# Prompt attention: value sums of two neighbouring key blocks issued as one run, six buffers of transposed weights, values loaded in pieces

## The chip, the cores and the metric

The kernel runs on one core of a Trainium2 chip. The metric is the device time of one launch in microseconds (us), as the median of three runs.

## The reference

One hybrid decoder layer for a prompt of 2048 tokens and for 32 sample tokens (8 sequences of 4). The layer normalises its input, multiplies it by one wide projection, feeds four groups (convolution, pooling, stick-breaking attention, attention to memory tokens), gates each, projects the result back and adds it to the residual. The change is in the stick-breaking attention of the prompt, 8 heads of 64:

```python
def sb_block(q, k, v, bias, q_pos, k_pos):
    z = (jnp.einsum('nqhd,nkhd->nhqk', q, k).astype(jnp.float32) * (SB_HEAD_DIM ** -0.5)
         + bias.astype(jnp.float32)[None, :, None, None])
    mask = (k_pos[None, :] < q_pos[:, None])[None, None]
    log_beta = jax.nn.log_sigmoid(z)
    log_1m = jnp.where(mask, jax.nn.log_sigmoid(-z), 0.0)
    rc = lax.cumsum(log_1m, axis=3, reverse=True)
    a = jnp.exp(jnp.where(mask, log_beta + rc - log_1m, -jnp.inf))
    return jnp.einsum('nhqk,nkhd->nqhd', a.astype(v.dtype), v)
```

In products instead of logarithms: the weight of a key is sigmoid(z) times the product of sigmoid(-z) over all later keys that the query may see.

## The kernel before

The kernel first projects the prompt and the sample tokens, with the sample's attention to its cache interleaved, then does prompt attention (about 1502 to 1990 us of the profile), and then the output projection. Queries, keys, values and gates go through DRAM scratch (`qd`, `kd`, `vd`, `gsd`) between the first two.

Prompt attention goes over 16 blocks: 4 head pairs `hp` by 4 query blocks `qb` of 512 tokens. Within a block it goes over key blocks `kc` of 512 from the diagonal down to 0, so there are 40 (block, `kc`) groups. Each group has four steps: two heads `hh` by two halves `q2` of the query block. The work of a step by engine:

- PE, `score` (L1248): four matmuls into a two-bank PSUM tile `S` (two buffers).
- ACT (L1253, L1255): two sigmoids of `S`, into `gam` (three tiles, used in turn) and `be`.
- DVE (L1265 on the diagonal, L1268 off it): two reversed running products of `gam` into `E`, with the carry from the key block before.
- POOL (L1277): two products of `be` and `E`, into `be`.

These two last parts (`rest`) are issued two steps after their score. Then, from a list sorted by step:

- `turn` (L1288): for each of four 128-key blocks `r` and each head, up to four PE transposes of the weights into a PSUM tile `AT` (two buffers), and a copy to the SBUF tile `at`, by ACT off the diagonal (L1294), by DVE with the mask on it (L1292). Both heads of block `r` go at step `base + r + 6`, where `base` is the group's first step.
- `values` (L1304): for block `r`, one product with the values for each head, the two heads side by side in halves of 64 columns of the array, all added into one PSUM tile `av` (one buffer). Each product is two PE instructions, so a call gives four. It goes at `base + r + 8`. After the last block of `kc` 0, DVE multiplies `av` by the gate `sgt` into `sbo` (L1309), and a DMA stores it.

The order of PE's instructions is that of the program (`manual_schedule` for PE). Those of the other engines and of the DMA queue are laid out by the framework's scheduler, which also sets the waits. Within one step of the sorted list older entries come first: values of block `r` come ahead of the transposes of block `r + 2`.

`load` (L1195 to L1211) is called one block ahead. It loads `Q` and `kT` of the block, and, at the first query block of a head pair, all 2048 tokens of the pair's values as one 1 MB tile `V` (two buffers). All of these DMAs are on SP's queue. Other work (sample attention to memory, the rest of the convolution, weights of the output projection) is mixed in through a generator of side work that takes its turns by the costs that `sb_prompt` yields; it uses ACT, DVE, POOL and SP, and the `AT` tiles.

Of the kernel before, what the change touches and what calls it, by code (L numbers as in the profile page):

```python
# [8 lines left out]
F32 = mybir.dt.float32  # L9
# [9 lines left out]
P = 128  # L19
# [39 lines left out]
SEND = 0.97  # L59
XA = 3  # L60
KT = 2
WR = 2


# [22 lines left out]
def kernel(  # L87
# [9 lines left out]
    pe, act, dve, pool, sp = nc.tensor, nc.scalar, nc.vector, nc.gpsimd, nc.sync  # L97
# [22 lines left out]
    vd = dram.tile([SEQ, 512], F32, name="vd")  # L120
# [7 lines left out]
    def mix_rows(ct, t0, n):  # L128

        return mixd[ct // 4, t0 // P : (t0 + n) // P, :, ct % 4].rearrange("b p t -> p b t")  # L130

    def by_tile(t):
        return t.rearrange("p (b t) -> p b t", t=P)
# [88 lines left out]
    def load_w(it):  # L222
        part, kind, c = it
        src, o = (w_mem0, P * c) if kind == "mem" else (w_in0, G[kind] + P * c)
        raw_ = wp.tile([P, ND, P], F32, tag="wr", name="wr%d%s%d" % it, bufs=WR)
        wq.dma_start(raw_, src[:, o : o + P].rearrange("(d p) n -> p d n", p=P))
        return raw_

    def split_w(raw, nm):
        lo = wp.tile([P, ND, P], F32R, tag="wlo", name=f"wlo{nm}", bufs=2)  # L230
        hi = wp.tile([P, ND, P], F32R, tag="whi", name=f"whi{nm}", bufs=2)
        act.copy(hi, raw)
        pool.tensor_tensor(out=lo, in0=raw, in1=hi.bitcast(F32), op=ALU.subtract)
        return hi, lo
# [505 lines left out]
    def next_raw():  # L740
        if SEQ_W:
            it = SEQ_W.pop(0)
            raw[it] = load_w(it)

    def fill_w(n=2):

        while len(wsplit) < n and (raw or SEQ_W):
# [3 lines left out]
            wsplit[it] = split_w(raw.pop(it), "%d%s%d" % it)  # L751
        while n == 2 and len(raw) < WR and SEQ_W:
            next_raw()
# [137 lines left out]
    def gather(dst, rows, idx):  # L891
        pool.indirect_dma_start(out=dst, out_offset=None, in_=rows, in_offset=bass.IndirectOffsetOnAxis(ap=idx, axis=0))  # L892

    def sample_stages(sm, sps, S):
# [8 lines left out]
        def page(n, ml):  # L903
            return NPAGE - 2 - 2 * (n % NCK) + ml

        def load_k(n, ml):
            if n < N:
                kt = sm.tile([P, 4 * 512], F32, tag="kt", name=f"kt{n}_{ml}", bufs=KT)
                gather(kt, krows, S["idk"][:, n // NCK, page(n, ml) : page(n, ml) + 1])
# [281 lines left out]
    def sb_loader(sbr):  # L1191

        KT, V = {}, {}

        def load(hp, qb):  # L1195
            tok = slice(512 * qb, 512 * qb + 512)
            Q = []
            for hh in range(2):
                pr = slice(64 * hh, 64 * hh + 64)
                kt = sbr.tile([P, 512], F32R, tag="kT", name=f"kT{hp}_{qb}_{hh}", bufs=10)  # L1200
                qt_ = sbr.tile([P, 2, 512], F32R, tag="Q", name=f"Q{hp}_{qb}_{hh}", bufs=4)
                for x in range(2):
                    hx = slice(64 * x, 64 * x + 64)
                    sp.dma_start(kt[hx].bitcast(F32), kd[hp, pr, x, tok])
                    sp.dma_start(qt_[hx].bitcast(F32), qd[hp, pr, :, tok])
                KT[hp, hh, qb] = kt
                Q.append(qt_)
            if qb == 0:
                V[hp] = sbr.tile([P, 16, P], F32, tag="V", name=f"V{hp}", bufs=2)
                sp.dma_start(V[hp], vd[:, P * hp : P * (hp + 1)].rearrange("(t p) c -> p t c", p=P))  # L1210
            return Q, KT, V[hp]  # L1211

        return load

    def sb_prompt(load, loaded, sb, bps, ops, flags):
# [18 lines left out]
        A, avs, ats = {}, {}, {}  # L1234
        count = {"pair": 0}

        def score(hp, qb, kc, hh, q2, Q, KT, carry):

# [7 lines left out]
            for j in range(2):  # L1246
                for x in range(2):
                    pe.matmul(S[:, j, :w], lhsT=Q[hh][:, x, P * (q2 + j) : P * (q2 + j + 1)], rhs=KT[hp, hh, kc][:, :w],  # L1248
                              start=x == 0, stop=x == 1)
# [32 lines left out]
        def turn(hp, qb, kc, r, hh):  # L1282
            dg = kc == qb
            q0 = r if dg else 0
            nm = f"{hp}_{qb}_{kc}_{r}_{hh}"
            ap_ = bps.tile([P, 512], F32, tag="AT", name=f"AT{nm}", bufs=2)
            for qt in range(q0, 4):
                pe.transpose(ap_[:, P * qt : P * (qt + 1)], A[hp, qb, kc, hh, qt][:, P * r : P * (r + 1)], ident)  # L1288
            at = sb.tile([P, 512], F32, tag="at", name=f"at{nm}", bufs=4)
            c = slice(P * q0, 512)  # L1290
            if dg:
                dve.tensor_tensor(out=at[:, c], in0=ap_[:, c], in1=tri[:, : 512 - P * q0], op=ALU.mult)  # L1292
            else:
                act.copy(at[:, c], ap_[:, c])  # L1294
            ats[hp, qb, kc, r, hh] = at

        def values(hp, qb, kc, r, V, gt):
            dg = kc == qb
            c = slice(P * r if dg else 0, 512)
            if dg and r == 0:  # L1300
                avs[hp, qb] = bps.tile([P, 512], F32, tag="av", name=f"av{hp}_{qb}", bufs=1)
            av = avs[hp, qb]
            for hh in range(2):
                pe.matmul(av[64 * hh : 64 * hh + 64, c], lhsT=V[:, 4 * kc + r, 64 * hh : 64 * hh + 64],  # L1304
                          rhs=ats.pop((hp, qb, kc, r, hh))[:, c], start=dg and r == 0, stop=kc == 0 and r == 3,
                          tile_position=(0, 64 * hh))
            if kc == 0 and r == 3:
                mo = sb.tile([P, 512], F32, tag="sbo", name=f"sbo{hp}_{qb}", bufs=1)
                dve.tensor_tensor(out=mo, in0=av, in1=gt, op=ALU.mult)  # L1309
                (pool if (hp, qb) == blocks[-1] else sp).dma_start(mix_rows(8 + hp, 512 * qb, 512), by_tile(mo))  # L1310
                flags.add((hp, qb))

        late, pend = [], []
        step = 0

        def behind(limit):
            while late and late[0][0] <= limit:
                late.pop(0)[1]()

        for bi, (hp, qb) in enumerate(blocks):  # L1320
            if bi + 1 < len(blocks) and blocks[bi + 1] not in loaded:
                loaded[blocks[bi + 1]] = load(*blocks[bi + 1])
            Q, KT, V = loaded[hp, qb]
            gt = sb.tile([P, 512], F32, tag="sgt", name=f"sgt{hp}_{qb}", bufs=1)
            sp.dma_start(gt, gsd[hp, :, 512 * qb : 512 * qb + 512])
            carry = {}
            for kc in range(qb, -1, -1):
                base = step
                for hh in range(2):
                    for q2 in (0, 2):  # L1330
                        cost = 1.33 * (2 * q2 + 3) / 4 if kc == qb else 2.66
                        rest = score(hp, qb, kc, hh, q2, Q, KT, carry)
                        if len(pend) == 2:
                            pend.pop(0)()
                        pend.append(rest)
                        yield cost / 2
                        behind(step)
                        step += 1
                        yield cost / 2
                for r in range(4):  # L1340
                    late.append((base + r + 6, lambda a=(hp, qb, kc, r, 0): turn(*a)))
                    late.append((base + r + 6, lambda a=(hp, qb, kc, r, 1): turn(*a)))
                    late.append((base + r + 8, lambda a=(hp, qb, kc, r, V, gt): values(*a)))
                late.sort(key=lambda x: x[0])
        flags.add("last")
        while late:
# [453 lines left out]
    sbr = bx = None  # L1800
    for cost in main():
        tasks.step()
        due += rate * cost
        while sample is not None and due >= 1.0:
            due -= 1.0
            try:
# [5 lines left out]
                sbr = bx.enter_context(tc.tile_pool(name="sbr", bufs=1, side="right", reuse_waits="tile"))  # L1812
# [5 lines left out]
    sb = bx.enter_context(tc.tile_pool(name="sbl", bufs=1, side="right", reuse_waits="tile"))  # L1818
# [81 lines left out]
    for cost in sb_prompt(load, blk, sb, bps, ops, flags):  # L1900
        steps += 1
        if steps > SLATE:
            due += cost
            while side is not None and due >= PACE:
                due -= PACE
                try:
                    next(side)
                except StopIteration:
                    side = None
        if "last" in flags and side is None:  # L1910
            if lead is None:
                os_.close()
                accp = oy.enter_context(tc.tile_pool(name="oacc", bufs=1, space=PSUM, side="left", reuse_waits="tile"))
                lead = leading()
            for _ in range(LPACE):
                next(lead, None)
# [148 lines left out]
```

## Time and profile before

| | us |
|---|---|
| median of 3 runs | 2429.65 (2429.42 to 2430.13) |
| profiled execution, span from the first to the last instruction | 2426.4 |
| what the median has beside that span | 3.25 |
| of it prompt attention, first score matmul to last value matmul | 1502.8 to 1990.5 |

The profile is of one execution. PE is the tensor engine's matmuls, PEld its weight loads, which overlap matmuls; DVE, ACT, POOL and SP are the vector, scalar, GpSimd and sync engines. A timeline row has the start and length in us, the engine, the line, the instruction, the tiles out<-in, the shapes, the number of like instructions merged into the row, and, in brackets, the idle time of the engine ahead of it with what ended that time. Instructions of PE and ACT overlap their neighbours, so the pace of an engine is read from start to start and not from the lengths.

### The profile page before, as it was taken

Reading aid. Unit: us, or ns where it says so; the run is one execution under the profiler, and the core shown is the slowest. Engines: PE = TensorE matmul, PEld = TensorE weight load, DVE = VectorE, ACT = ScalarE, POOL = GpSimd, SP = SyncE. Lnnn points to the kernel's source line nnn. Section 1 sums busy time; section 2 is a strip of 40 time slices with the busy share of each in tenths; the row PEclk is TensorE's granted clock in tenths of the full one; section 3 lists DMA queues with packets and bytes.
Section 4 is the critical chain, followed back from the end, with each engine's and each line's share of the span. In section 5 each row is a group of like instructions: output and inputs, shape, how many; then the busy total and the mean of one; then the engine's idle time right before and its main releaser. Section 6 shows DMA issues by size and latency. Waiting matters only on the chain. (4 is left out here: it accounts for less than half of the span.)

```text
span 2426.4 us, 42151 instructions
## 1 busy us (share of the span) xinstructions
PE 2290.7 (94%) x15962; PEld 1776.1 (73%) x15962; DVE 1736.2 (72%) x2434; ACT 1118.5 (46%) x1939; POOL 1272.7 (52%) x1309
## 2 busy tenths in 40 slices
PE   6999999999999999999999999899999998989997
PEld 6998888898887777777777776455555556777775
DVE  5332784969756665477877877888898857886898
ACT  5322343242442322124241425688989955543444
POOL 2554545556574455655555554576876844433330
PEclk9999999999999999999999999999999999999998
DMA  5678988887778799987877776834332227887764
GB/s 184 213 253 285 350 290 292 290 263 265 261 253 275 271 346 329 312 285 253 290 265 271 260 239 164 239 81 118 101 88 73 63 63 239 272 279 254 238 240 161
DMA packets 340438, 562.15 MB, mean 232 GB/s; under 512 B 28481, under 2 KB 212929, under 8 KB 323834
## 3 DMA queue, kind: packets, MB, share of 16 engines
q1 hardware_dynamic: 284858, 290.72, 39.1%
q0 software_dynamic: 55376, 268.72, 31.1%
q8 instruction: 126, 2.06, 0.3%
q14 instruction: 78, 0.64, 0.1%
HBM read 469.28 MB, written 90.68 MB: 231 GB/s over the span
## 5 line engine op out<-in xcount | busy, mean ns | idle before, releaser
L925 DVE STREAM_TRANSPOSE T<-kt 128x1024 f32<-128x1024 f32 x256 | 308.8, 1226 | 193.6 <-PE sSA L938 183.0
L892 POOL DMA_INDIRECT vt<-in_cache_v_dram,idv x256 | 250.4, 978 | 239.7 <-PE sO L977 178.8
L583 DVE SCALAR_TENSOR_TENSOR cacc<-U,par,cacc 128x512 f32<-128x512 f32 x480 | 360.1, 750 | 11.8
L1277 POOL TENSOR_TENSOR be<-be,E 128x512 f32<-128x512 f32 (+2 forms) x320 | 303.5, 956 | 117.0 <-DVE E L1268 52.6
L1268 DVE TENSOR_TENSOR_SCAN E<-gam,cr,ZM 128x513 f32<-128x513 f32 x192 | 232.9, 1262 | 14.4 <-ACT gam L1253 13.2
L892 POOL DMA_INDIRECT kt<-in_cache_k_dram,idk x128 | 125.6, 981 | 206.9 <-DVE T L925 152.5
L1288 PEld LDWEIGHTS AT<-ident,be 128*128 128x128 f32 x1088 | 117.9, 142 | 127.3 <-ACT at L1294 45.3
L1885 PE MATMUL acc<-wohi,mh 128*128 128x512 f32 (+1 forms) x480 | 193.6, 403 | 3.9 <-DVE mh L1650 2.0
L1253 ACT ACTIVATE gam<-S,nbias_bc 128x1024 f32<-128x1024 f32 (+1 forms) x160 | 172.5, 1078 | 51.2 <-ACT be L1255 18.9
L1885 PE MATMUL acc<-wolo,mh 128*128 128x512 f32 (+1 forms) x480 | 190.8, 397 | 0.0
L1885 PE MATMUL acc<-wohi,ml 128*128 128x512 f32 x448 | 179.2, 400 | 12.1 <-DVE ml L1650 12.1
L1248 PE MATMUL S<-kT,Q 128*128 128x512 f32 (+1 forms) x640 | 177.9, 401 | 6.1 <-ACT be L1255 2.6
L1288 PE MATMUL AT<-ident,be 128*128 128x128 f32 x1088 | 158.4, 284 | 13.8 <-DVE at L1292 3.9
L1255 ACT ACTIVATE be<-S,bias_bc 128x1024 f32<-128x1024 f32 (+1 forms) x160 | 171.4, 1071 | 0.0
L1304 PE MATMUL av<-at,V 128*64 128x512 f32 (+3 forms) x640 | 153.0, 557 | 1.7 <-DVE sbo L1309 1.7
L938 PE MATMUL sSA<-T,W 128*32 128x128 f32 x4096 | 140.8, 277 | 7.6 <-DVE T L925 6.4
L938 PEld LDWEIGHTS sSA<-T,W 128*32 128x32 f32 x4096 | 105.4, 110 | 44.9 <-issue 37.2
L977 PE MATMUL sO<-vt,saT 128*32 128x512 f32 x1024 | 123.7, 597 | 0.0
L1248 PEld LDWEIGHTS S<-kT,Q 128*128 128x128 f32 x640 | 107.3, 196 | 22.2 <-ACT be L1255 3.5
L1650 DVE TENSOR_TENSOR ml<-mr,mh 128x512 fp32r<-128x512 f32 x108 | 97.0, 905 | 33.6 <-ACT mh L1639 33.4
L1265 DVE TENSOR_TENSOR_SCAN E<-gam,ZM 128x128 f32<-128x128 f32 (+3 forms) x128 | 96.4, 802 | 29.3 <-ACT gam L1253 22.3
L1294 ACT COPY at<-AT 128x512 f32<-128x512 f32 x192 | 109.0, 656 | 14.4 <-PE AT L1288 14.4
(571 smaller groups left out, 6032.8 us busy)
## 6 DMA issues: line engine op xcount, KB each, us to landing
Q<-qd SPq DMA_DIRECT2D x64, 256.0 KB
mr<-mixd SPq DMA_DIRECT2D x32, 512.0 KB
mr<-mixd SPq DMA_DIRECT2D x48, 256.0 KB
wor<-in_w_out_dram SPq DMA_DIRECT2D x20, 512.0 KB
xtp<-in_x_prompt_dram SPq DMA_DIRECT2D x16, 512.0 KB
kT<-kd SPq DMA_DIRECT2D x64, 128.0 KB
wor<-in_w_out_dram SPq DMA_DIRECT2D x32, 256.0 KB
msd<-mr SPq DMA_DIRECT2D x32, 256.0 KB
```

Source lines behind the costliest of these rows:

```text
L583: dve.scalar_tensor_tensor(out=ps, in0=U[:, a + k : a + k + H], scalar=wd[:, k : k + 1], in1=ps, op0=ALU.mult, op1=ALU.add)
L892: pool.indirect_dma_start(out=dst, out_offset=None, in_=rows, in_offset=bass.IndirectOffsetOnAxis(ap=idx, axis=0))
L925: dve.transpose(T[:, 2 * hh : 2 * hh + 2].rearrange("p s j t -> p (s j t)"), kt[:, 2 * hh : 2 * hh + 2].rearrange("p s j d -> p (s j d)"))
L938: pe.matmul(sSs[n][32 * g : 32 * g + 32, P * ml : P * (ml + 1)], lhsT=W[:, jj, :], rhs=T[:, :, jj, :], start=i == 0, stop=i == 3, tile_pos ...
L1248: pe.matmul(S[:, j, :w], lhsT=Q[hh][:, x, P * (q2 + j) : P * (q2 + j + 1)], rhs=KT[hp, hh, kc][:, :w], start=x == 0, stop=x == 1)
L1253: act.activation(out=ga[:, :, 512 - w : 512], in_=S[:, :, :w], func=AF.Sigmoid, bias=nbias_bc[:, h : h + 1], scale=-1.0)
L1255: act.activation(out=be[:, :, :w], in_=S[:, :, :w], func=AF.Sigmoid, bias=bias_bc[:, h : h + 1])
L1268: dve.tensor_tensor_scan(out=E[:, j][:, ::-1], data0=ga[:, j][:, ::-1], data1=ZM[:, 0:1].to_broadcast([P, 513]), initial=carry[hh, q2][:, ...
L1277: pool.tensor_tensor(out=be[:, j, :m], in0=be[:, j, :m], in1=E[:, j, 513 - w : 513 - w + m], op=ALU.mult)
L1288: pe.transpose(ap_[:, P * qt : P * (qt + 1)], A[hp, qb, kc, hh, qt][:, P * r : P * (r + 1)], ident)
L1304: pe.matmul(av[64 * hh : 64 * hh + 64, c], lhsT=V[:, 4 * kc + r, 64 * hh : 64 * hh + 64], rhs=ats.pop((hp, qb, kc, r, hh))[:, c], start=dg ...
L1885: pe.matmul(o[:rows], lhsT=m[a][:, k, :rows], rhs=W[prod, 4 * h + k][w], start=not cont and h == k == n == 0, stop=h == 1 and k == 3 and n ...
```

## The change

A call of `values` now takes two neighbouring blocks `r2` and `r2 + 1` and issues their eight PE instructions as one run, at the step at which the second of them went before (`base + 9` and `base + 11`). The first block of each pair therefore comes one step later. `at` has six buffers in place of four. The values come in one 256 KB piece of 512 tokens for each block (`V`, six buffers of 2 KB a partition, in place of two of 8 KB), loaded with the block's `Q` and `kT`, so the `V` tiles take 4 KB a partition less and the `at` tiles 4 KB more.

```diff
+ATB = 6
...
-            if qb == 0:
-                V[hp] = sbr.tile([P, 16, P], F32, tag="V", name=f"V{hp}", bufs=2)
-                sp.dma_start(V[hp], vd[:, P * hp : P * (hp + 1)].rearrange("(t p) c -> p t c", p=P))
-            return Q, KT, V[hp]
+            V[hp, qb] = sbr.tile([P, 4, P], F32, tag="V", name=f"V{hp}_{qb}", bufs=6)
+            sp.dma_start(V[hp, qb], vd[tok, P * hp : P * (hp + 1)].rearrange("(t p) c -> p t c", p=P))
+            return Q, KT, V
...
-            at = sb.tile([P, 512], F32, tag="at", name=f"at{nm}", bufs=4)
+            at = sb.tile([P, 512], F32, tag="at", name=f"at{nm}", bufs=ATB)
...
-        def values(hp, qb, kc, r, V, gt):
+        def values(hp, qb, kc, r2, V, gt):
             dg = kc == qb
-            c = slice(P * r if dg else 0, 512)
-            if dg and r == 0:
+            if dg and r2 == 0:
                 avs[hp, qb] = bps.tile([P, 512], F32, tag="av", name=f"av{hp}_{qb}", bufs=1)
             av = avs[hp, qb]
-            for hh in range(2):
-                pe.matmul(av[64 * hh : 64 * hh + 64, c], lhsT=V[:, 4 * kc + r, 64 * hh : 64 * hh + 64],
-                          rhs=ats.pop((hp, qb, kc, r, hh))[:, c], start=dg and r == 0, stop=kc == 0 and r == 3,
-                          tile_position=(0, 64 * hh))
-            if kc == 0 and r == 3:
+            for r in (r2, r2 + 1):
+                c = slice(P * r if dg else 0, 512)
+                for hh in range(2):
+                    pe.matmul(av[64 * hh : 64 * hh + 64, c], lhsT=V[hp, kc][:, r, 64 * hh : 64 * hh + 64],
+                              rhs=ats.pop((hp, qb, kc, r, hh))[:, c], start=dg and r == 0, stop=kc == 0 and r == 3,
+                              tile_position=(0, 64 * hh))
+            if kc == 0 and r2 == 2:
...
-                    late.append((base + r + 8, lambda a=(hp, qb, kc, r, V, gt): values(*a)))
+                    if r % 2:
+                        late.append((base + r + 8, lambda a=(hp, qb, kc, r - 1, V, gt): values(*a)))
```

## The prediction

> **What bounds the kernel now.** I read the page first, then the stretches of prompt attention one head pair at a time, then the timelines of one step by engine, and last the waits.
>
> ```profile
> span 2426.4 us, 42151 instructions
> PE 2290.7 (94%) x15962; PEld 1776.1 (73%) x15962; DVE 1736.2 (72%) x2434; ACT 1118.5 (46%) x1939; POOL 1272.7 (52%) x1309
> ```
>
> The span is 2426.4 us; the median of the three runs is 2429.65, so 3.25 us lie around the span, and I leave them as they are. PE is busy 94%, but that mean hides what matters here. The change touches only prompt attention, which runs from about 1502 to 1990 us. The windows give it per head pair; the first three are (columns: length, then busy time and count of PE, PEld, DVE, ACT, POOL, granted clock, DMA share, GB/s):
>
> ```profile
> 1502.00:1627.00 125.00, 109.18 (x627) 62.74 (x628) 101.12 (x132) 94.85 (x119) 81.14 (x121) 0.93 0.66 177
> 1627.00:1743.00 116.00, 110.08 (x612) 64.94 (x611) 100.09 (x132) 103.22 (x140) 87.28 (x113) 0.97 0.40 101
> 1743.00:1852.00 109.00, 105.84 (x597) 61.86 (x595) 96.13 (x117) 99.15 (x129) 78.74 (x105) 1.00 0.34 86
> ```
>
> In the third row, the cleanest (109 us for 40 steps, 2.72 us a step), PE is busy 97%, but DVE 88% and ACT 91% too. Three engines run nearly level. So what PE gives up is worth something only where PE alone is late. The PE timeline of one stretch shows the step:
>
> ```profile
> 1841.31 1.08 PE L1304 MATMUL av<-at,V 128*64 128x512 f32 x4
> 1842.32 1.09 PE L1288 MATMUL AT<-ident,be 128*128 128x128 f32 x8
> 1843.17 1.17 PE L1248 MATMUL S<-kT,Q 128*128 128x512 f32 x4
> 1844.27 1.08 PE L1304 MATMUL av<-at,V 128*64 128x512 f32 x4
> ```
>
> From one `av` to the next is 2.96 us: 1.01 for four value matmuls, 0.85 for eight transposes, 1.10 for four score matmuls (each up to the start of the next row). None of these rows has idle time before it. ACT in the same stretch:
>
> ```profile
> 1842.34 1.19 ACT L1253 ACTIVATE gam<-S,nbias_bc 128x1024 f32<-128x1024 f32 x1
> 1843.35 1.18 ACT L1255 ACTIVATE be<-S,bias_bc 128x1024 f32<-128x1024 f32 x1
> 1844.34 1.14 ACT L1294 COPY at<-AT 128x512 f32<-128x512 f32 x2
> 1845.28 1.22 ACT L1253 ACTIVATE gam<-S,nbias_bc 128x1024 f32<-128x1024 f32 x1
> ```
>
> Start to start that is 1.01 + 0.99 + 0.94 = 2.94 us, with nothing idle: here ACT is full as well, 0.02 us behind PE. DVE is full elsewhere. These are the places in the third head pair where the DVE timeline shows idle time ahead of an instruction (the last number), after a long stretch without any:
>
> ```profile
> 1764.87 0.69 DVE L1309 TENSOR_TENSOR sbo<-av,sgt 128x512 f32<-128x512 f32 x1 [0.19 <-PE av L1304]
> ...
> 1789.07 2.46 DVE L1268 TENSOR_TENSOR_SCAN E<-gam,cr,ZM 128x513 f32<-128x513 f32 x2 [0.70 <-ACT gam L1253]
> 1792.06 2.46 DVE L1268 TENSOR_TENSOR_SCAN E<-gam,cr,ZM 128x513 f32<-128x513 f32 x2 [0.53 <-ACT gam L1253]
> ...
> 1818.13 2.07 DVE L1265 TENSOR_TENSOR_SCAN E<-gam,ZM 128x384 f32<-128x384 f32 x2 [1.55 <-ACT gam L1253]
> ...
> 1827.38 1.29 DVE L1292 TENSOR_TENSOR at<-AT,tri 128x512 f32<-128x512 f32 x2 [0.83 <-PE AT L1288]
> ...
> 1852.57 2.46 DVE L1268 TENSOR_TENSOR_SCAN E<-gam,cr,ZM 128x513 f32<-128x513 f32 x2 [0.17 <-POOL be L1277]
> ```
>
> DVE runs without a listed pause from 1764.9 to 1788.4, from 1792.1 to 1816.6 and from 1827.4 to 1852.4: 73 of 109 us. These stretches begin where the masked copies of a diagonal block (L1292) join the scans. There PE already waits, for instance here:
>
> ```profile
> 1782.62 1.22 PE L1288 MATMUL AT<-ident,be 128*128 128x128 f32 x8 [1.25 <-DVE at L1292]
> ```
>
> **The merged value runs.** The page has the work:
>
> ```profile
> L1304 PE MATMUL av<-at,V 128*64 128x512 f32 (+3 forms) x640 | 153.0, 557 | 1.7 <-DVE sbo L1309 1.7
> ```
>
> 640 matmuls in runs of four are 160 runs; the change makes 80 runs of eight. No matmul goes away. What goes is half the entries into and exits from the 128*64 form. By luck the trace already holds one run of eight, at the end of attention, where the last two value sums stand side by side:
>
> ```profile
> 1985.88 1.08 PE L1304 MATMUL av<-at,V 128*64 128x512 f32 x4
> 1986.89 1.09 PE L1288 MATMUL AT<-ident,be 128*128 128x128 f32 x8
> 1987.74 0.48 PE L1885 MATMUL acc<-wohi,mh 128*128 128x512 f32 x1
> 1988.05 0.40 PE L1885 MATMUL acc<-wolo,mh 128*128 128x512 f32 x1
> 1988.29 0.40 PE L1885 MATMUL acc<-wohi,ml 128*128 128x512 f32 x1
> 1988.61 1.94 PE L1304 MATMUL av<-at,V 128*64 128x512 f32 x8
> 1990.48 0.50 PE L1885 MATMUL acc<-wohi,mh 128*128 128x512 f32 x1
> ```
>
> A run of four holds PE for 1986.89 - 1985.88 = 1.01 us, the run of eight for 1990.48 - 1988.61 = 1.87. Merging saves 2 x 1.01 - 1.87 = 0.15 us inside. Outside, the last 512-column matmul ahead of the run takes 1988.61 - 1988.29 = 0.32 until `av` starts, against 1988.29 - 1988.05 = 0.24 between two of one form: another 0.08. The step without values then goes from scores straight to transposes; the trace hardly shows that order undisturbed, so its price stands between 0 and another 0.06 gained (some exposed weight load). I take 0.02, near the lower end, since the rows show no more: 0.25 us a merge, bounds 0.15 to 0.30. Over 80 merges PE gives up 20 us (12 to 24).
>
> The weights of the later pairs could be a catch. In that run of eight:
>
> ```profile
> 1989.10 0.14 PEld L1304 LDWEIGHTS av<-at,V 128*64 128x64 f32 x2 [0.29 <-issue]
> 1989.53 0.14 PEld L1304 LDWEIGHTS av<-at,V 128*64 128x64 f32 x2 [0.28 <-issue]
> ```
>
> Loads of 0.14 us stand at 1989.10 and 1989.53, 0.43 us apart, in the middle of a matmul run that ends only at 1990.48, so they lie under matmuls. The Trainium skill ("TensorE: Matmul & The Clock Gate", Part 3, The mechanism) says that a weight load overlaps matmuls in flight only when its row group differs; these all use 128 rows. By that rule a load would be exposed at the joint of two merged runs, and more than half of the gain would go (rival 4). The trace speaks against it here.
>
> **How much of it shows.** In the third head pair DVE has slack in 109 - 73 = 36 us, minus a few where ACT is just as full: about 33 us, 12 steps, 6 merges. I count those in full: 6 x 0.25 = 1.5 us. The other 14 merges lie in stretches where DVE or ACT is full; some queue slack stands between the engines, so the end of such a stretch can still come a little earlier. Bounds 0 and 0.25; I take 0.09, nearer the full engines than PE: 1.26 us. That is 2.75 us a head pair, so 5.5 for the last two, taking the fourth like the third. In the first two, PE is busy 87% and 95% because other work makes it wait; I take 1.0 and 1.5. Sum: 8.0 us.
>
> **Six buffers of `at`.** With the pairing, block 0 of a pair waits one step longer, so six `at` tiles live at once: blocks 0, 1, 2 of two heads. With four, the copy of block 2 would wait. With six, the tile that block 3 takes is freed by the value run that PE issues just ahead of block 3's own transposes, so no wait is added. Cost nothing; if that cover failed, a copy would wait for a value run of at most 1.87 us.
>
> **The longer step.** Steps now alternate: 2.96 + 0.86 with eight value matmuls, 2.96 - 1.01 without. In a long step the transposes come 0.86 us later after their scores, and their copies stand in ACT's order ahead of the next `gam`. In the full stretch above the transposes that started at 1842.32 finish their first half by about 1842.8 and their copy started only at 1844.34: 1.5 us of slack, more than 0.86. In the short step the next transposes need the `AT` tiles back after only the scores' 1.10 us instead of 2.11, and wait where ACT lags; over two steps ACT's 5.88 us then decides.
>
> **Values in pieces.** Bytes are equal: 16 x 256 KB for 4 x 1 MB. SP issues 12 more transfers:
>
> ```profile
> 1649.35 0.38 SPq L1210 DMA_DIRECT2D V<-vd x1
> ```
>
> and from the waits over 1500 to 1990 us and those of SP's queue:
>
> ```profile
> PE S L1248 <- DMA Q<-qd: 2.0, 2, 1.4
> ...
> SPq L1325 <- DVE sbo L1309: 86.7, 11, 26.1
> ...
> SPq L1210 <- PE AT L1288: 19.2, 2, 11.0
> ```
>
> 12 x 0.38 us is 4.6 us on a queue that stands 86.7 us waiting for `sbo` alone. The third piece of head pairs 2 to 4 reuses the tile of the first piece of the pair before, which is free only when that pair's last value run has ended: three waits where now two cost SP 19.2 us, at the same moment (the 1 MB load issued at 1649.35 is one of the two, kept by the first head pair's values). Queued behind are `sgt`, which waits for `sbo` anyway, and Q and kT of the next blocks. PE lost 2.0 us to Q in all of attention, so I take nothing, bounds +5 (a Q late by half a 9.6 us wait, once) and -2 (the first 1 MB transfer no longer ahead of the first Qs). The first value run of a block comes a step later, so its wait for `sbo` (1.7 us in the page's row) may go; it lies in full DVE stretches, so nothing.
>
> **Sum.** 2426.4 - 8.0 + 3.25 = 2421.65 us. The output projection behind attention starts where attention ends; I let it shift whole.
>
> **Rivals.** (1) PE alone sets the pace. For it: no PE idle in the step above. Against: ACT's 2.94 and DVE's 73 us. It gives 80 x 0.30 = 24 us, 2405.7. (2) The other engines take it all: DVE and ACT stretches grow into the gaps and only 0 to 3 us are left: 2428. For it: DVE 88%, ACT 91%. Against: DVE idles for 1.55 and 0.83 us waiting for work that PE feeds. (3) Slower: in the stretches where ACT is full, the transposes of the long step come 0.86 us later and ACT, in order, stands idle for its copies. It decides from the point where the slack ahead of a copy is below 0.86 us. With 6 such merges a head pair, 24 in all, and 0.86 - 0.25 = 0.61 us lost in each, 14.6 us go, less 6.0 us won in the 24 free merges: 8.6 us slower, 2438.3. Against it: the 1.5 us of slack read off above. (4) The second half of a merged run cannot load its weights under the first half, so that one load of 0.14 us (the PEld rows) is exposed at each joint: 0.25 - 0.14 = 0.11 us a merge, 8.0 x 0.11 / 0.25 = 3.5 us, 2426.1. The loads inside the run of eight speak against it. The Trainium skill's rule on row groups, named above, would have it so.
>
> **How the numbers follow.** What a measurement of this kernel can tell from no change is 0.2%, 4.9 us. Chances: forecast 0.55 (its own range 2415 to 2427), rival 1 0.10, rival 2 0.16, rival 3 0.15, rival 4 0.04. Faster by over 4.9 us (below 2424.8): 0.85 of the forecast and rival 1, 0.57. Same: rivals 2 and 4, the rest of the forecast and a little of rival 3, 0.28. Slower (above 2434.5): 0.15 with the SP bound. The range 2410 to 2436 takes in the forecast, rivals 2 and 4 and the near side of rival 3, and leaves out the far ends of rivals 1 and 3.
>
> **What would show it.** Right: `av` rows of x8 about 1.87 us long from start to start, rows that go S to AT without `av` between, and a pair of steps near 5.67 us where DVE and ACT are free but 5.88 where ACT is full; the third head pair at about 106 us instead of 109; DVE's pauses on ACT and PE shorter. Wrong: pairs of steps at 5.92 with new PE idle on "ACT at" or "DVE at" (rival 2), ACT idle before its copies in long steps (rival 3), all pairs near 5.62 (rival 1), an x8 run of 2.02 us (rival 4), or S waiting for Q behind a V piece.

## The result: 0.7% slower, 2446.2 us against 2429.5

The changed kernel takes 2446.18 us (2445.67 to 2448.09) against 2429.53 us before; the ratio is 1.0070 with a 95% interval of 1.0053 to 1.0086. The forecast was 2421.7 us. From here on "attention" is the time from the first score matmul to the start of the last value matmul in one profile. What stands ahead of it takes some us more or less from run to run with the same code (attention starts at 1495.1 to 1502.8 us in the profiles below), while attention itself comes out alike: 487.2 us in the kernel before, 486.2 us in a version that differs from it only in buffers and loads. So attention is taken as the finer measure, and ratios of whole times are given beside it. Each figure of attention is of one execution, and how far it moves from one to the next was not measured, so a difference of a few us in it is not firm.

The page after, first two lines and the groups of the transposes and of the value matmuls:

```profile
span 2444.3 us, 42120 instructions
...
PE 2278.8 (93%) x15962; PEld 1777.5 (73%) x15962; DVE 1741.5 (71%) x2434; ACT 1120.8 (46%) x1939; POOL 1279.9 (52%) x1309
...
L1288 PE MATMUL AT<-ident,be 128*128 128x128 f32 x1088 | 159.6, 283 | 41.1 <-DVE at L1292 24.8
...
L1305 PE MATMUL av<-at,V 128*64 128x512 f32 (+3 forms) x640 | 137.9, 552 | 0.0
```

PE is busy 11.9 us less than before, and the value matmuls are 15.1 us of that (153.0 to 137.9, 0.19 a merge). Yet the span is 17.9 us longer. The idle time ahead of the transposes has risen from 13.8 to 41.1 us, and most of it ends with DVE's masked copy `at` (L1292). By head pair, from the first score matmul of a pair to that of the next, attention takes 134.4, 118.1, 114.9 and 142.1 us. The window of the third pair (columns as in the table of the prediction):

```profile
1750.10:1865.00 114.90, 104.83 (x596) 63.52 (x594) 97.03 (x117) 99.42 (x129) 79.03 (x105) 0.99 0.33 81
```

In the same cut the kernel before has 124.3, 116.3, 108.7 and 137.9 us. Attention takes 509.5 us in place of 487.2: 22.3 us more, spread over all four head pairs. What follows attention takes 437.2 us against 436.4. The waits of PE from 1495 to 2015 us, before and after (columns: total us, times, longest):

```profile
PE AT L1288 <- DVE at L1292: 3.9, 4, 1.2
PE AT L1288 <- ACT at L1294: 3.8, 6, 1.1
```

```profile
PE AT L1288 <- DVE at L1292: 24.8, 20, 1.9
...
PE AT L1288 <- ACT at L1294: 5.7, 14, 1.0
```

The wait for DVE to empty an `AT` tile grew by 20.9 us, the one for ACT by 1.9. The timeline of PE in the third head pair, from the group `qb` 2, `kc` 0, in which the last masked copies of the diagonal fall:

```profile
1803.70 1.94 PE L1305 MATMUL av<-at,V 128*64 128x512 f32 x8
1805.57 0.88 PE L1288 MATMUL AT<-ident,be 128*128 128x128 f32 x6
1806.20 1.18 PE L1248 MATMUL S<-kT,Q 128*128 128x512 f32 x4
1808.48 0.90 PE L1288 MATMUL AT<-ident,be 128*128 128x128 f32 x4 [1.10 <-DVE at L1292]
...
1812.09 1.17 PE L1248 MATMUL S<-kT,Q 128*128 128x512 f32 x4
1814.76 1.06 PE L1288 MATMUL AT<-ident,be 128*128 128x128 f32 x8 [1.49 <-DVE at L1292]
...
1818.33 0.71 PE L1248 MATMUL S<-kT,Q 128*128 128x256 f32 x4
```

The run of eight is 1805.57 - 1803.70 = 1.87 us, as forecast. But the four steps from 1806.20 to 1818.33 take 12.13 us, where the kernel before needs 9.94, and two waits for DVE of 1.10 and 1.49 us stand in them. DVE at the same time:

```profile
1802.58 1.26 DVE L1292 TENSOR_TENSOR at<-AT,tri 128x512 f32<-128x512 f32 x2
1803.76 3.62 DVE L1268 TENSOR_TENSOR_SCAN E<-gam,cr,ZM 128x513 f32<-128x513 f32 x3
1807.30 0.67 DVE L1310 TENSOR_TENSOR sbo<-av,sgt 128x512 f32<-128x512 f32 x1
1807.88 1.50 DVE L1292 TENSOR_TENSOR at<-AT,tri 128x384 f32<-128x384 f32 x3
1809.30 1.27 DVE L1268 TENSOR_TENSOR_SCAN E<-gam,cr,ZM 128x513 f32<-128x513 f32 x1
1810.49 0.40 DVE L1292 TENSOR_TENSOR at<-AT,tri 128x256 f32<-128x256 f32 x1
1810.81 3.62 DVE L1268 TENSOR_TENSOR_SCAN E<-gam,cr,ZM 128x513 f32<-128x513 f32 x3
```

DVE has no idle time here; it does other things first. Between the 512-column masked copies and the 384-column ones stand three scans, and three more ahead of the last, 128-column ones. The kernel before has two and two at the same place:

```profile
1794.66 1.29 DVE L1292 TENSOR_TENSOR at<-AT,tri 128x512 f32<-128x512 f32 x2
1795.86 2.44 DVE L1268 TENSOR_TENSOR_SCAN E<-gam,cr,ZM 128x513 f32<-128x513 f32 x2
1798.22 0.67 DVE L1309 TENSOR_TENSOR sbo<-av,sgt 128x512 f32<-128x512 f32 x1
1798.81 1.01 DVE L1292 TENSOR_TENSOR at<-AT,tri 128x384 f32<-128x384 f32 x2
...
1801.57 2.45 DVE L1268 TENSOR_TENSOR_SCAN E<-gam,cr,ZM 128x513 f32<-128x513 f32 x2
1803.93 0.46 DVE L1292 TENSOR_TENSOR at<-AT,tri 128x128 f32<-128x128 f32 x2
```

No line of the change speaks of DVE's order: the framework lays that queue, and with the value runs at other places it laid it anew.

### The profile page after: what moved, and what is told of

It is laid out like the page before. It is cut to its first block, busy times and chain, and to the rows that moved or that the text cites. A ratio compares the mean times of both kernels' runs of the same rounds, so it can differ in the third digit from the quotient of the medians.

```text
span 2444.3 us, 42120 instructions
## 1 busy us (share of the span) xinstructions
PE 2278.8 (93%) x15962; PEld 1777.5 (73%) x15962; DVE 1741.5 (71%) x2434; ACT 1120.8 (46%) x1939; POOL 1279.9 (52%) x1309
## 5 line engine op out<-in xcount | busy, mean ns | idle before, releaser
L1268 DVE TENSOR_TENSOR_SCAN E<-gam,cr,ZM 128x513 f32<-128x513 f32 x192 | 234.3, 1265 | 24.5 <-ACT gam L1253 22.0
L1288 PE MATMUL AT<-ident,be 128*128 128x128 f32 x1088 | 159.6, 283 | 41.1 <-DVE at L1292 24.8
L1305 PE MATMUL av<-at,V 128*64 128x512 f32 (+3 forms) x640 | 137.9, 552 | 0.0
L1294 ACT COPY at<-AT 128x512 f32<-128x512 f32 x192 | 106.0, 623 | 18.4 <-PE AT L1288 17.2
```

The costliest lines, as they stand in the source:

```text
L1268: dve.tensor_tensor_scan(out=E[:, j][:, ::-1], data0=ga[:, j][:, ::-1], data1=ZM[:, 0:1].to_broadcast([P, 513]), initial=carry[hh, q2][:, ...
L1305: pe.matmul(av[64 * hh : 64 * hh + 64, c], lhsT=V[hp, kc][:, r, 64 * hh : 64 * hh + 64], rhs=ats.pop((hp, qb, kc, r, hh))[:, c], start=dg ...
```

## The experiments

Two theories stood: (A) DVE's queue was laid in a worse order; (B) the new rhythm of long and short steps costs time by itself, since in a short step both `AT` tiles are wanted back early. The rival to both was that the pieces of V or the six buffers cost the time.

| kernel | attention us | ratio to before | 95% interval |
|---|---|---|---|
| before | 487.2 | | |
| after | 509.5 | 1.0070 | 1.0053 to 1.0086 |
| e1 pieces and six buffers, nothing merged | 486.2 | 0.9997 | 0.9986 to 1.0008 |
| e2 after, DVE's order as before | 496.4 | 1.0045 | 1.0030 to 1.0059 |
| e3 before, DVE's order as after | 513.7 | 1.0137 | 1.0117 to 1.0158 |
| e8 pairs in one step, not merged, DVE's order as before | 507.4 | 1.0075 | 1.0058 to 1.0093 |
| e9 merged between the heads, DVE's order as before | 511.2 | 1.0111 | 1.0092 to 1.0130 |
| e10 ten of twenty runs a head pair merged, DVE's order as before | 485.8 | 0.9986 | 0.9972 to 0.9999 |
| e11 six of twenty merged, DVE's order as before | 489.1 | 0.9997 | 0.9983 to 1.0011 |
| e12 e11 with DVE's order left to the framework | 496.9 | 1.0026 | 1.0013 to 1.0038 |

### Pieces and buffers alone, and DVE's order changed over

e1 is the changed kernel with the values taken one block a call, at `base + r + 8`, as before:

```diff
-                    if r % 2:
-                        late.append((base + r + 8, lambda a=(hp, qb, kc, r - 1, V, gt): values(*a)))
+                    late.append((base + r + 8, lambda a=(hp, qb, kc, r, V, gt): values(*a)))
```

e2 and e3 fix the order of DVE's scans (E), masked copies (t) and gate products (s) in attention by dependencies without a semaphore. `DVE_ORDER` is the order read off the other kernel:

```diff
+        queue = [dv[k].pop(0).ins for k, n in re.findall(r"([Ets])(\d*)", DVE_ORDER) for _ in range(int(n or 1))]
+        for x, y in zip(queue, queue[1:]):
+            tc.add_manual_dep(y, x.name, mybir.DependencyInfo(mybir.DependencyClass.NoSync, mybir.DependencyReason.DATA),
+                              reason="order")
```

For one diagonal block the order before reads "t2 E2 s t2 E t2 E2 t2", the order after "t2 E3 s t3 E t E3 t2".

> The change without its merging: values in 256 KB pieces and six at buffers, but each value sum issued by itself at its old step; PE order and (but for two rows) DVE order are those of before. If DVE's new order or the long step costs the 17 us, this stands at 2429 +-4 us. If the pieces (more transfers and waits on SP's queue) cost it, 2437 to 2446.

> The whole change, with the order of DVE's scans, masked copies and gate products held to that of before by edges. Order theory (the scheduler moved a scan ahead of the masked copies of each diagonal block, PE waits for the copies): the loss goes and the merging shows, 2418 to 2428, near 2422. Rhythm theory (transposes after a run of eight come too late for whatever order): 2440 to 2447. Half of each: near 2434.

> The kernel before, with DVE's scans, masked copies and gate products held to the order that they have in the changed kernel. Order theory: slower by most of the 17 us and the merging's unseen gain, 2440 to 2450. Rhythm theory: within 4 us of before, as PE still gives the transposes early.

Measured: e1 486.2 us of attention, so pieces and six buffers cost nothing that shows. e2 496.4 us: of the 22.3 us, 13.1 come back with DVE's order. e3 513.7 us: the new order alone, in the old kernel, costs 26.5 us. The whole times expected were for a kernel before at 2429.5 us; beside these three runs it took 2421.6. Against that, e2 is 10.9 us slower (7 to 14), near the lower end of what the rhythm theory gave, and e3 33 us, more than the 10 to 20 of the order theory.

That e3 loses twice the 13.1 us shows in a second wait of PE. The third scan stands ahead of the gate product too, which empties `av` for PE's next value run:

```profile
PE AT L1292 <- DVE at L1296: 16.6, 11, 2.0
PE av L1308 <- DVE sbo L1313: 16.3, 13, 1.8
```

In the kernel before, the wait for `sbo` is 1.7 us. In the changed kernel the first value run of a block comes a step later, and the wait is 0.0. The same group as above, in e2, PE and then DVE:

```profile
1799.62 1.18 PE L1251 MATMUL S<-kT,Q 128*128 128x512 f32 x4
1800.72 0.90 PE L1292 MATMUL AT<-ident,be 128*128 128x128 f32 x4
...
1804.33 1.18 PE L1251 MATMUL S<-kT,Q 128*128 128x512 f32 x4
1805.65 1.06 PE L1292 MATMUL AT<-ident,be 128*128 128x128 f32 x8
...
1809.22 0.71 PE L1251 MATMUL S<-kT,Q 128*128 128x256 f32 x4
```

```profile
1795.99 1.26 DVE L1296 TENSOR_TENSOR at<-AT,tri 128x512 f32<-128x512 f32 x2
1797.17 2.45 DVE L1271 TENSOR_TENSOR_SCAN E<-gam,cr,ZM 128x513 f32<-128x513 f32 x2
1799.53 0.67 DVE L1314 TENSOR_TENSOR sbo<-av,sgt 128x512 f32<-128x512 f32 x1
1800.11 1.01 DVE L1296 TENSOR_TENSOR at<-AT,tri 128x384 f32<-128x384 f32 x2
```

With two scans ahead of the 384-column copies, the transposes at 1800.72 have no wait, and the group takes 1809.22 - 1799.62 = 9.60 us: 2.53 less than after, and 0.34 less than before (two merged runs, 0.17 each). Theory A is shown, in both directions: PE's instructions stand in the same order in each of the two pairs of kernels, and ACT's and POOL's but for a few places. It is not the whole: e2 is still 9.2 us behind the kernel before. Its waits name another engine first:

```profile
PE AT L1292 <- ACT at L1298: 12.7, 24, 1.8
PE AT L1292 <- DVE at L1296: 8.3, 10, 1.8
```

In e1 these are 3.7 and 4.6 us. One of them in e2, on PE and on ACT:

```profile
1841.51 1.09 PE L1292 MATMUL AT<-ident,be 128*128 128x128 f32 x8
1842.35 1.17 PE L1251 MATMUL S<-kT,Q 128*128 128x512 f32 x4
1844.34 1.14 PE L1292 MATMUL AT<-ident,be 128*128 128x128 f32 x8 [0.82 <-ACT at L1298]
```

```profile
1842.67 1.15 ACT L1258 ACTIVATE be<-S,bias_bc 128x1024 f32<-128x1024 f32 x1
1843.67 1.11 ACT L1298 COPY at<-AT 128x512 f32<-128x512 f32 x2
1844.61 1.19 ACT L1256 ACTIVATE gam<-S,nbias_bc 128x1024 f32<-128x1024 f32 x1
```

The transposes of 1841.51 fill both `AT` tiles. ACT, busy without a gap, copies them only from 1843.67, and PE, which in a short step has just the scores in between, stands still for 0.82 us. That step takes 2.89 us (1842.35 to 1845.24), 2.07 without the wait.

### A third AT tile: the question stays open

To test theory B by a third `AT` tile, a PSUM bank was needed. The zero row `ZM`, the scans' second operand, was moved from PSUM to SBUF for it, with five V buffers for six. e4 is the control (e1 with that move, two `AT` tiles, DVE's order as before), e5 has three tiles, e6 is e2 with three, e7 is the changed kernel with three and the framework's own order.

```diff
-        ZM = bps.tile([P, 512], F32, name="ZM", bufs=1)
+        ZM = sb.tile([P, 512], F32, name="ZM", bufs=1)
...
-            ap_ = bps.tile([P, 512], F32, tag="AT", name=f"AT{nm}", bufs=2)
+            ap_ = bps.tile([P, 512], F32, tag="AT", name=f"AT{nm}", bufs=3)
```

> Control for the next two: pieces without merging, DVE order of before, the zero row ZM moved from PSUM to SBUF (which gives one PSUM bank free) and five V buffers in place of six. Both theories: same attention span as before, 487 +-2 us from first score to last value matmul; more if scans that read ZM from SBUF are slower or collide with POOL.

> The same with a third AT buffer in PSUM, still unmerged. Rhythm theory: little, as in an even rhythm two buffers were enough: 0 to 4 us less attention than the control. If AT buffers bound the kernel before as well, 5 us or more less.

> The whole change with DVE's order of before, ZM in SBUF and three AT buffers. With two it had 496 us of attention against 487. If the rest of the loss is the short step's transposes waiting for AT buffers that ACT or DVE give back late, three buffers bring it to 478 to 487 us (a merge saves PE 0.15 us, 80 merges 12 us at most). If the rest is the late transposes of the long step, a third buffer changes little: 493 to 497.

> The changed kernel with ZM in SBUF, five V buffers and three AT buffers, and DVE's order left to the scheduler, which with a third buffer mostly lays two scans, not three, between the masked copies. Order theory with the rhythm theory: between the last kernel and the changed one, 480 to 500 us of attention, not 509.

Measured: e4 1.0555 (1.0534 to 1.0576), attention 621.1 us; e5 1.0511 (1.0492 to 1.0531), 610.7; e6 1.0519 (1.0501 to 1.0536), 615.0; e7 1.0533 (1.0509 to 1.0557), 615.8. The control alone is 134.9 us of attention slower than e1. Its groups, then those of e1:

```profile
L1281 POOL TENSOR_TENSOR be<-be,E 128x512 f32<-128x512 f32 (+2 forms) x320 | 447.6, 1421 | 41.4 <-DVE E L1271 23.3
...
L1271 DVE TENSOR_TENSOR_SCAN E<-gam,cr,ZM 128x513 f32<-128x513 f32 x192 | 348.9, 1866 | 6.9 <-ACT gam L1256 4.6
```

```profile
L1277 POOL TENSOR_TENSOR be<-be,E 128x512 f32<-128x512 f32 (+2 forms) x320 | 303.5, 956 | 117.0 <-DVE E L1268 54.1
L1268 DVE TENSOR_TENSOR_SCAN E<-gam,cr,ZM 128x513 f32<-128x513 f32 x192 | 233.1, 1265 | 13.8 <-ACT gam L1253 12.2
```

A scan goes from 1265 to 1866 ns and POOL's product from 956 to 1421 ns. PE's transposes wait 45.7 us for POOL's products, 0.4 in e1. So e5 is 10.4 us of attention below e4, but DVE and POOL set much of the pace in all four, and what a third tile is worth to PE in the changed kernel can't be read from them. e4 came out as the end of its expectation said (more if the scans are slower or collide with POOL), e6 and e7 over 100 us above theirs. The question stays open.

### The rhythm without the merging, and the run at another place

e8 keeps the long and the short step but merges nothing: in the long step it goes values of block r, transposes of head 0, values of block r + 1, transposes of head 1. e9 puts the merged run between the transposes of the two heads. Both have DVE's order as before. The list entries of e8, and the one of e9 that differs (with `turn` at + 6 and + 6.5). In both, a step now takes all entries below the next whole number, so that the parts behind the point order the work within a step:

```diff
-            while late and late[0][0] <= limit:
+            while late and late[0][0] < limit + 1:
...
+                    late.append((base + r + 6.2, lambda a=(hp, qb, kc, r, 0): turn(*a)))
+                    late.append((base + r + 6.6, lambda a=(hp, qb, kc, r, 1): turn(*a)))
+                    late.append((base + r + (8.4 if r % 2 else 9), lambda a=(hp, qb, kc, r, 1, V, gt): values(*a)))
...
+                        late.append((base + r + 8.25, lambda a=(hp, qb, kc, r - 1, V, gt): values(*a)))
```

> Both value sums of a pair stay in the step where the merged run stands, but transpositions of one head lie between them (first sum, transpositions of head 0, second sum, transpositions of head 1): nothing is merged, the long and the short step remain, and VectorE has the order of the kernel before. If the rhythm of long and short steps costs the time that was left when VectorE's order was put back (attention 496.4 us against 487.2, with a merging gain of 80 x 0.15 = 12 us inside it), attention takes 500 to 508 us here, ScalarE's late copies hold up TensorE's transpositions for about 12 us as there, and the ratio is 1.005 to 1.009. If the cost lies in the unbroken run of eight itself (transpositions and scores late by its 1.9 us), the run is broken here and attention takes about 487 us, the ratio 0.998 to 1.001.

> The merged run of eight stays, but stands between the transpositions of head 0 and those of head 1 in the long step, VectorE in the order of the kernel before. If the cost of the rhythm is that in the short step both transposed buffers are asked for again 2.0 us after they were filled, one of the two now gets longer in each gap: waits for ScalarE's copies fall from 12.7 to 5 to 9 us and attention from 496.4 to 489 to 494 us, ratio 1.001 to 1.003. If the copies come late since ScalarE is full, whichever buffer is asked for, nothing changes: 495 to 498 us, ratio 1.004 to 1.006.

Measured: e8 507.4 us, inside what theory B gave and 20 us from its rival: the unbroken run of eight is not what costs. Merging the two runs of e8 (that is e2) takes 11.0 us away again, 0.14 a merge. But e8 isn't the rhythm alone. It parts the eight transposes of a long step by a value run, and where no engine waits this shows: their two halves take 0.59 and 0.41 us there (from 1855.49 to 1856.08 and from 1857.09 to 1857.50 in its profile) where the undivided eight took 0.85. The group with `kc` 1 of `qb` 3 (third head pair) takes 9.94 us in e1, 9.63 in e2 and 10.21 in e8. That is 0.27 for two pairs, 0.14 each, up to 11 of e8's 21.2 us. What is left, 10 us or more, is put down to the rhythm. Most of it falls in the same three groups of a head pair as in e2 (third head pair, `qb`, `kc`): (2,2) 10.18 us in e1, 12.01 in e2, 11.17 in e8; (3,3) 11.22, 12.05, 12.23; (3,0) 11.84, 12.76, 12.66. These three lose 3.6 us in e2 and 2.8 in e8, and the other seven together win 1.4 in e2 and lose 1.8 in e8.

e9 went against both expectations. Its waits:

```profile
PE AT L1292 <- ACT at L1298: 21.8, 27, 1.4
...
PE AT L1292 <- DVE at L1296: 11.9, 14, 1.4
```

It was to relieve one of the two tiles, and the waits for ACT rose from 12.7 to 21.8 us. ACT's timeline there shows a reason:

```profile
1858.02 0.69 ACT L1298 COPY at<-AT 128x512 f32<-128x512 f32 x1
1858.98 0.59 ACT L1298 COPY at<-AT 128x512 f32<-128x512 f32 x1 [0.27 <-PE AT L1292]
```

The transposes of the second head now come after the run of eight. ACT, in whose queue their copy stands ahead of the next sigmoids, idles for them: 0.27 us here. There are 38 such waits in attention (14.2 us) against 7 in e2 (13.4 us). That is a bit of time lost on an engine that has none to spare; how much of e9's loss it makes is not shown.

### Merging only where it won

e10 merges ten of a head pair's twenty runs, those that fall in groups which e2 had made shorter; e11 six. e12 is e11 without the fixed order of DVE.

```diff
+MERGED = {(1, 0), (2, 2), (2, 0), (3, 3), (3, 0)}
...
+                    n = 2 if (qb, kc) in MERGED else 1
+                    if r % n == n - 1:
+                        late.append((base + r + 8, lambda a=(hp, qb, kc, r - n + 1, n, V, gt): values(*a)))
```

> Only those blocks are merged whose value runs fell, with VectorE in the old order, into stretches that became shorter: the blocks (1,0), (2,2), (2,0), (3,3), (3,0) of each head pair, 10 merged runs of 20; the others keep a value sum a step. If each stretch's gain or loss is its own (0.14, 0.34, 0.17, 0.30 us and nothing for the five), a head pair gains about 1 us and attention takes 481 to 485 us against 486.2 with no merging: ratio 0.997 to 0.999. If the gains were only paid for by stretches next to them (work that is late there catches up here), attention takes 485 to 490 us and the ratio is 1.000 +- 0.0015.

> Value sums merged in the blocks (2,2), (2,0) and (3,3) of each head pair alone (6 of 20 runs), VectorE in the order of the kernel before. With ten runs merged, the stretches in which these six fall were 0.32, 0.16 and 0.31 us shorter per head pair and one next to another of the ten was 0.48 us longer. If gain and loss belong to the stretch in which a run falls, attention takes 486.2 - 4 x 0.8 = 483 us (482 to 484.5), and the ratio to the kernel before is 0.997 to 0.999. If work that is late there only catches up elsewhere, attention takes 485 to 487 us, ratio 0.999 to 1.001.

> The same six merged runs, but the order of VectorE's queue left to the framework. It puts a third scan ahead of the gate product or of the second masked copies in 8 of the diagonal blocks instead of the 12 of the whole change. If that order costs what it did with all runs merged (13.1 us over the whole), attention takes 5 to 10 us longer than with the order of the kernel before: 488 to 494 us, ratio 1.001 to 1.004. If the order only costs together with the long and short steps, both kernels agree within 2 us and the ratio is 0.997 to 1.000.

Measured: e10 485.8 us, 0.4 less than without any merging, and the only kernel whose interval lies below 1, at 0.9986 (0.9972 to 0.9999): by a hair, and less than the 0.2% that the prediction called a difference. Both of its figures are in the range that was given for gains which the next stretch pays for. e11, meant to keep e10's gains without its one loss, came out at 489.1 us, above both of its ranges. The 3.3 us between the two lie in the first two head pairs, where other work is mixed in: 124.2 and 114.2 us in e10, 125.7 and 116.5 in e11. Whether the merging has to do with that is not shown. The third pair takes 108.7 us in the kernel before, in e1 and in e10, and 108.9 in e11, so nothing is won there. Its groups show how: in e10, (2,1) had lost 0.48 us (12.10 for 11.62) and (2,0), the next, had won 0.32 (9.62). In e11 (2,1) is back at 11.62 and (2,0) is at 10.36, worse than without merging. The sum of the two is 21.72 and 21.98 us, against 21.56 in e1. So the won group goes with a lost one, as late work would that catches up, and the two together win nothing. What remains of merging in both is 0.16 us in (3,2) and 0.31 in (3,1) of a head pair, less 0.10 in (3,3) and 0.1 in (0,0).

e12 is 7.8 us of attention behind e11, within the 5 to 10 expected. PE and ACT have the same order in both, POOL but for two places; what differs is DVE's order, and again by a third scan. Its group (3,1) takes 12.13 us, to the hundredth what it takes in the kernel after, against 9.63 in e11, and the waits, of e11 and of e12, are

```profile
PE AT L1293 <- DVE at L1297: 8.1, 12, 1.2
PE AT L1293 <- ACT at L1299: 5.3, 13, 1.1
```

```profile
PE AT L1289 <- DVE at L1293: 18.7, 17, 1.5
...
PE AT L1289 <- ACT at L1295: 1.9, 6, 0.6
```

## Why the prediction was wrong

The parts of the 22.3 us, each the difference of two of the kernels above: pieces and buffers -1.0 (e1 less before), pairing the value sums in one step +21.2 (e8 less e1, up to 11 of it the parted transposes that e8 adds), merging them -11.0 (e2 less e8), DVE's new order +13.1 (after less e2). The parts are in this order and would shift in another: the DVE order costs 26.5 us in the old rhythm (e3). Nor are their sizes firm. By the whole times (the ratios times 2421 us) the change costs 17 us (13 to 21), and the same four parts are -1, +19, -7 and +6. The profile of e2 is of the second fastest of its twelve runs (2424.4 us, median 2430.6), so what DVE's order costs in the changed kernel is 13 us by one measure and 6 by the other. That it costs is plain from e3 and from e12 against e11. The prediction had given a slower kernel a chance of 0.15; the 2446.2 us lie above all the times that it worked out.

- **Right: the run of eight.** 1.87 us, as read off the one such run at the end of attention. Weights of the second half cost nothing, so rival 4 is out. The Trainium skill's rule ("TensorE: Matmul & The Clock Gate", Part 3, The mechanism), as the prediction read it (only loads of another row group overlap), does not hold for these loads: the measurement decides. The same section of the Trainium skill also lets loads into the background weight buffer go ahead of matmuls in flight, which the prediction left out; no run here shows where these loads went.
- **Right: values in pieces, six buffers, and the output projection shifting whole.** e1 is within 1.0 us of attention, PE does not wait for Q any more (2.0 us before), and what follows attention differs by 0.8 us (428.1 to 438.5 us in all the profiles).
- **Mis-sized: the merge.** 0.25 us was taken, with bounds of 0.15 to 0.30. The groups without waits show 0.15 to 0.17. The 0.08 for the entry did not come: in e2's group (3,3) of the third head pair a short step without a wait takes 1.50 us where it took 2.51 in e1, less by 1.00, about the 1.01 of a run, and the long one behind it 3.81 where it took 2.96, more by about the 0.86 of the second half. The 0.06 that the prediction allowed above that had no row behind it. But all this is at most 8 us over 80 merges, and not the sign.
- **The first failed step: "How much of it shows".** It bounded the merges in DVE-full stretches at 0 from below, as if DVE did the same work in the same order. The prediction had no term for DVE's queue being laid anew. What the runs showed in its place is a third scan ahead of the masked copies: PE's wait for DVE went from 3.9 to 24.8 us. Nothing in the trace of before shows what the framework will do, but the trace did show what a scan more ahead of a masked copy is worth: PE already waited there for 1.25 us, and one scan takes 1.18 us from start to start. As an estimate, sixteen diagonal blocks with two such places each put up to 32 x 1.18 = 38 us within reach, so that the term's bound should have lain far below zero.
- **The second failed step: "The longer step".** It named the mechanism, the `AT` tiles wanted back after 1.10 us in the short step, and then priced it at nothing, since over two steps ACT's 5.88 us is below 5.92. Where ACT's queue is full, that average does not hold. In e2's group (3,0) of the third head pair ACT runs at its 2.94 us a step, and two pairs of steps take 12.76 us, 6.38 each. The long steps take 3.84 us, as summed (3.82), but the short ones take 2.89 and 2.19 in place of 1.95, and 0.82 us of that is the wait for the copy shown above. So the loss is all in the short step. That PE can't use time which it won ahead of a full ACT is the reading of this; no run takes it apart. The 1.5 us of slack was read for the long step's copies, which were not the ones that came too late.
- **Rivals.** Rival 3 had the sign, and about half of the size (2438.3), but another carrier: PE waits for copies, not ACT for transposes (ACT's wait for transposes is 13.4 us in e2, 14.4 in e1, 17.2 in the changed kernel). Its mechanism appears in e9, and perhaps in e8 (18.9 us, 25 waits). The sign named for rival 2, new idle time of PE that ends with the copies of DVE and ACT, is what came; the rival itself, that the others take all of the gain, is what e10 and e11 come to once DVE's order is held fixed and the rhythm left mostly alone.

Open: how large the part left in e2 is (9 us by attention, 11 by whole times), and how it divides between the short step's two tiles and ACT being full, since the run that was to give PE a third tile was overtaken by the moved zero row; and by what costs the framework came to put a third scan first.

## What to carry to other kernels

Where another program lays an engine's queue, a change to one engine's order can change the others too: compare the order of the full engines first, and hold it fixed to see what the edit itself does. Where three engines run nearly level, a saving on one must be read as a change of rhythm: ask which buffer is now wanted back sooner, and price a short and a long step each by itself, not by their mean. Where a stretch gets shorter next to one that gets longer, count the two together.

## What the hardware showed beside this

Moving a scan's constant second operand from PSUM to SBUF made the scan 1.48 times as long (1265 to 1866 ns) and POOL's products, whose own operands did not move, 1.49 times (956 to 1421 ns): 134.9 us of attention between e1 and e4. Besides, e4 has one V buffer less and DVE's order held; with the order held and `ZM` in PSUM (e2) a scan takes 1265 ns. The Trainium skill ("SBUF — State Buffer", Who interferes with whom) has a rule for it: a vector instruction with two SBUF inputs takes its second through the read port that GpSimd reads by, and the one that comes second waits. The trace agrees in that both engines' instructions got longer; how long each waited is not to be seen in it. The changes between the 128-column and the 64-column form of the array are cheap, about 0.14 to 0.17 us for a run of value matmuls joined to another or set between transposes.
